# Hybrid decoder layer on one core: the first four weight tiles accumulated together by k tile from a packed array

## The chip, the cores and the metric

The kernel runs on one core of a Trainium2 chip. The metric is the time of one execution on the device in microseconds (us); the time of a version is the median of its runs. The engines are named as the profile names them: PE (TensorE's matmuls), PEld (its weight loads), DVE (VectorE), ACT (ScalarE), POOL (GpSimd) and SP, whose queue issues most DMAs.

## The reference

One decoder layer on x of 512 tokens by 1024 channels: a SwiGLU half-step, two token mixers side by side, cross-attention to a memory of 256 rows, a second SwiGLU half-step and a final norm. What matters here is the first line and the compression in the mixer:

```python
def swiglu(h, w_gate, w_up, w_down):
    return (jax.nn.silu(h @ w_gate) * (h @ w_up)) @ w_down

x = x + 0.5 * swiglu(rms_norm(x, norm_ffn1[l]), w1_gate[l], w1_up[l], w1_down[l])
...
    def compress(a, pe, w1, w2):
        blocks = a[:, tok] + pe[None, None, :, None, :]
        flat = blocks.transpose(0, 1, 3, 2, 4).reshape(B, n_cmp, G, CMP_BLOCK * HEAD_DIM)
        return jax.nn.gelu(flat @ w1) @ w2
```

D_FF is 2816, so gate and up have 22 tiles of 128 columns each. All is float32.

## The kernel before

Activations lie transposed: `x[k]`, k = 0 to 7, holds 128 channels by 512 tokens. Each float32 operand is split into a high part and a low remainder (`h` and `l`), and a product is the sum of three matmuls: high by high, high by low, low by high. A split takes one ACT copy (`h`) and one DVE subtraction (`l = src - h`). Weights arrive in raw tiles `wr` (3 buffers) and are split into pairs `wh`, `wl` (2 buffers of 128 x 1024); `wload` does load and split, and `dense` runs the matmuls of one output tile, k by k, into a PSUM bank. Bank tag "d" has three buffers, "s" and "t" two, "o" one.

The norm's factor is applied after the products: ACT multiplies x by the gain only (`xh`, `xl`), and the factor `rb`, one per token, comes from `Norm`: squares on ACT (`sq`), their sum on DVE (`acc`), column sums on PE (L189), a square root on ACT (L206), four small matmuls that spread it over the partitions (L218), and a copy (L221).

`ffn` first runs `nstd` standard feature tiles (6 in the first half-step, 4 in the second): gate tile f, then up tile f, 24 matmuls each. In the first half-step the loads of gate tile 0, up tile 0 and x are written out by hand on SP's queue (L146, L139), in pieces, since no work can start before them. Behind a gate tile DVE multiplies by `rb` (`t1`, L310), ACT takes silu, DVE multiplies by `rb` once more (L313), and behind the up tile DVE makes `act` (L316). `prepare` (after the tiles in `PREP`) makes the operands for the other 16 tiles, which `seven` runs as pairs of tiles with seven products of half the size each. Ahead of `seven` stand four filler matmuls into banks that nobody reads (L408). `seven` begins with the splits of pair 0: `h1` (1024 columns from the raw tile `r1`), the sum `s2`, then `h2` (two halves of 512). Its first product reads the first 512 columns of `h1`, its second the first 512 of `h2`, its third the second half of `h2`, its fourth the second half of `h1`.

In the mixer, `compress_in` makes a projection tile and spreads it over `F` with eight DVE additions, `fh` and `fl` being their splits; `keys` makes a projection tile and its splits `kkh`, `kkl`. They run in the order compress_in(0), compress_in(1), keys(3), keys(2), keys(4), and after them the value projection `vcat` (L726) fills three banks "d" and one "o". A bank "d" comes free when DVE has read it (`q32` in compress_in, printed as q; `zg` in keys).

The instructions between `ordered()` keep the order in which they are written. The rest is ordered by a scheduler at build time that goes by priorities; each engine then runs its own list strictly in order.

## Time and profile before

| what | value |
|---|---|
| median of 3 runs | 1271.76 us (1271.66 to 1272.06) |
| the profiled execution, its own time | 1270.87 us |
| its span from the first to the last instruction | 1268.9 us |
| PE busy | 1250.5 us, 99% of the span |
| DVE busy | 839.4 us, 66% |
| ACT busy | 664.7 us, 52% |
| granted TensorE clock, mean | 0.998 |
| mean DMA rate | 131 GB/s |

The profile is of one execution. Its own time stands 2.0 us above its span, and 0.9 us below the median of the runs. Matmuls are pipelined, so the busy time of one overlaps the next; how fast PE goes is read from the distance of two starts.

### The profile page before, as it was taken

How to read it: one execution, taken by the hardware profiler on the slowest of the kernel's cores; microseconds unless marked ns; L12 is line 12 of the kernel's file. 1: busy time of each engine (PE TensorE's matmuls, PEld its weight loads, DVE VectorE, ACT ScalarE, POOL GpSimd, SP SyncE). 2: the span in 40 equal slices, each digit the busy share in tenths (PEclk: the TensorE clock that was granted, in tenths of full speed). 3: DMA queues.
4: the chain of work that ended last, by engine and by line, in shares of the span. 5: the costliest groups of instructions: out<-in, count | busy, mean ns of one | idle time of the engine just before them, and what ended most of it. 6: DMA issues, size and time to landing. Idle time of an engine off the chain costs nothing.

```text
span 1268.9 us, 19130 instructions
## 1 busy us (share of the span) xinstructions
PE 1250.5 (99%) x7324; PEld 1092.2 (86%) x7324; DVE 839.4 (66%) x1642; ACT 664.7 (52%) x1309; POOL 74.8 (6%) x101
## 2 busy tenths in 40 slices
PE   7999999999999999999999999999999999999997
PEld 5889999987888788888888898887889999998887
DVE  5867676744357888787878666555687777674224
ACT  6345555632234777777785454444445545553223
POOL 0101110003010000000001000000001111100000
PEclk9999999999999999999999999999999999999999
DMA  5727767237542522222224335211446766623233
GB/s 186 192 81 205 187 175 191 86 121 222 179 157 90 183 80 75 88 65 72 64 91 149 134 128 188 81 53 67 125 132 163 184 189 190 181 80 99 86 102 112
DMA packets 58939, 166.01 MB, mean 131 GB/s; under 512 B 6264, under 2 KB 6784, under 8 KB 58848
## 3 DMA queue, kind: packets, MB, share of 16 engines
q1 hardware_dynamic: 44240, 129.16, 30.6%
q0 software_dynamic: 14032, 34.57, 12.6%
q8 instruction: 57, 0.93, 0.3%
q10 hardware_dynamic: 576, 1.07, 0.2%
q14 instruction: 34, 0.28, 0.1%
HBM read 160.54 MB, written 10.07 MB: 134 GB/s over the span
## 4 chain that ended last, share of the span: by engine, by line
PE 96%; DVE 2%; DMA 1%; issue 0%; ACT 0%; SPq 0%; DVEq 0%
PE ps_d L127 47%; PE ps_d L75 12%; PE ps_t L75 8%; PE ps_d L500 5%; PE ps_o L75 4%; PE ps_s L75 4%; PE ps_d L978 4%; PE ps_d L1132 2%; PE ps_t L863 1%; PE ps_s L776 1%; PE ps_o L771 1%; PE ps_s L775 1%; PE ps_o L770 1%; PE ps_d L726 1%; PE ps_o L1191 1%; PE ps_s L1165 1%
## 5 line engine op out<-in xcount | busy, mean ns | idle before, releaser
L102 ACT ACTIVATE wh<-wr 128x512 fp32r<-128x512 f32 (+3 forms) x257 | 170.0, 695 | 299.6 <-PE ps_d L127 154.1
L103 DVE TENSOR_TENSOR wl<-wr,wh 128x512 fp32r<-128x512 f32 (+3 forms) x257 | 191.9, 771 | 136.9 <-ACT wh L102 135.3
L127 PE MATMUL ps_d<-xh,wh 128*128 128x512 f32 x456 | 182.3, 401 | 7.3 <-ACT xh L75 7.3
L127 PE MATMUL ps_d<-xh,wl 128*128 128x512 f32 x456 | 183.3, 402 | 0.8 <-DVE wl L103 0.8
L127 PE MATMUL ps_d<-xl,wh 128*128 128x512 f32 x456 | 182.2, 400 | 0.2 <-DVE xl L75 0.2
L127 PEld LDWEIGHTS ps_d<-xh,wh 128*128 128x128 f32 x456 | 86.3, 189 | 25.8 <-ACT xh L75 9.1
L127 PE MATMUL ps_d<-al,wh 128*128 128x512 f32 (+1 forms) x286 | 107.8, 377 | 0.0
L127 PE MATMUL ps_d<-ah,wh 128*128 128x512 f32 (+1 forms) x286 | 107.8, 377 | 0.0
L127 PE MATMUL ps_d<-ah,wl 128*128 128x512 f32 (+1 forms) x286 | 107.7, 376 | 0.0
L127 PEld LDWEIGHTS ps_d<-xl,wh 128*128 128x128 f32 x456 | 86.3, 189 | 19.1 <-DVE xl L75 1.8
L127 PEld LDWEIGHTS ps_d<-xh,wl 128*128 128x128 f32 x456 | 86.4, 189 | 18.7 <-DVE wl L103 1.3
L75 DVE TENSOR_TENSOR wl<-wr,wh 128x1024 fp32r<-128x1024 f32 (+3 forms) x46 | 49.6, 1085 | 27.5 <-ACT wh L75 27.5
L127 PEld LDWEIGHTS ps_d<-al,wh 128*128 128x128 f32 x286 | 53.8, 188 | 10.6
L127 PEld LDWEIGHTS ps_d<-ah,wh 128*128 128x128 f32 x286 | 53.8, 188 | 10.5
L127 PEld LDWEIGHTS ps_d<-ah,wl 128*128 128x128 f32 x286 | 53.8, 188 | 10.4
L75 DVE TENSOR_TENSOR h4l<-r,h4h 128x1024 fp32r<-128x1024 f32 x34 | 41.7, 1226 | 19.5 <-ACT h4h L75 19.5
L75 DVE TENSOR_TENSOR h2l<-s,h2h 128x512 fp32r<-128x512 f32 x68 | 44.0, 687 | 14.0 <-ACT h2h L75 13.8
L75 PE MATMUL ps_d<-t,h4h 128*128 128x256 f32 x272 | 50.5, 283 | 0.0
L75 PE MATMUL ps_d<-n,h2h 128*128 128x256 f32 x272 | 50.4, 283 | 0.0
L75 PE MATMUL ps_o<-t,h2h 128*128 128x256 f32 x272 | 50.3, 283 | 0.0
L75 PE MATMUL ps_t<-n,h3h 128*128 128x256 f32 x272 | 49.9, 282 | 0.0
L75 PE MATMUL ps_t<-b,h4h 128*128 128x256 f32 x272 | 49.9, 281 | 0.0
(348 smaller groups left out, 3144.1 us busy)
## 6 DMA issues: line engine op xcount, KB each, us to landing
wr<-in_w_down_dram SPq DMA_DIRECT2D x34, 512.0 KB, 3.5
wr<-in_w_in_dram SPq DMA_DIRECT2D x29, 512.0 KB, 3.5
wr<-in_w_gate_dram SPq DMA_DIRECT2D x26, 512.0 KB, 5.2
wr<-in_w_up_dram SPq DMA_DIRECT2D x26, 512.0 KB, 5.8
s<-in_w_gate_dram SPq DMA_DIRECT2D x17, 512.0 KB, 5.1
s<-in_w_gate_dram POOLq DMA_DIRECT2D x17, 512.0 KB, 5.9
s<-in_w_up_dram SPq DMA_DIRECT2D x17, 512.0 KB, 5.0
s<-in_w_up_dram POOLq DMA_DIRECT2D x17, 512.0 KB, 5.8
```

The lines of the kernel that those rows point to most:

```text
L75: return lambda *args, **kw: tc.keep_in_program_order(call(*args, **kw))
L102: A.activation(h, src, AF.Copy)
L103: V.tensor_sub(l, src, f32(h))
L127: yield T.matmul(out, w[:, c], m, start=i == 0, stop=i == total - 1)
L500: T.matmul(two[m], w[:, cc], v, start=f == 0 and z == 0, stop=f == FT - 1 and z == 2)
L726: T.matmul(pv[i][:, :VC], m[k][:, tk], ww[:, w], start=k == 0 and z == 0, stop=k == KT - 1 and z == 2)
L770: T.matmul(po[:, cols], w, h[:, src], start=start, stop=False, skip_group_check=True)
L771: T.matmul(po[:, cols], w, l[:, src], start=False, stop=False, skip_group_check=True)
L775: first = T.matmul(out, q[:, tk], kk[0][:, ks], start=True, stop=False)
L776: T.matmul(out, q[:, tk], kk[1][:, ks], start=False, stop=True)
L978: yield T.matmul(pj, w[:, c], m, start=n == 0, stop=n == 11)
L1132: T.matmul(pj[t], m[k][:, tk], ww[:, w], start=k == 0 and z == 0, stop=k == KT - 1 and z == 2)
```

## The change

Four edits, cut to their core below. First, gate tiles 0 and 1 and up tiles 0 and 1 come from one array `w1_first`, four raw tiles of 128 x 1024, each with two k tiles of all four; they are accumulated k by k into two banks "d" and two "s", 12 matmuls for each k. x tiles are loaded between the packed tiles. Second, nine matmuls on a tile of zeros (`WARM`) go ahead of them. Third, `PREP` of the first half-step goes from (1, 3) to (2, 4), since tiles 0 and 1 now end together. Fourth, two orders: `seven` splits pair 0 by halves in the order in which products read them, in both half-steps, and keys(3) goes between the two compress_in.

```diff
-PREP = {"1": (1, 3), "2": (0, 1)}
+PREP = {"1": (2, 4), "2": (0, 1)}
 NEARLY = 4
+WARM = 9
...
-    load_w(0, 0, 256)
+    def load_w(i, c0=0, c1=1024):
+        if c0 == 0:
+            raw0.append(raw_tile())
+        nc.sync.dma_start(raw0[i][:, c0:c1], a["w1_first"][i][:, c0:c1])
+
+    load_w(0, 0, 512)
     load_x(0)
-    load_w(1, 0, 256)
+    load_w(0, 512, 1024)
     load_x(1)
-    load_w(0, 256, 1024)
-    load_x(2)
-    load_w(1, 256, 1024)
-    for k in range(3, KT):
-        load_x(k)
+    for i in range(1, 4):
+        load_w(i)
+        load_x(2 * i)
+        load_x(2 * i + 1)
...
-            pg, pu = bank("d"), bank("d")
-            fg, fu = first if first and f == 0 else (None, None)
-            dense(pg, [(wsrc["g"][f], KT)], xh, xl, fg, step=1024)
+            if first and f < 2:
+                pg, pu = first[2 * f:2 * f + 2]
+            else:
+                pg, pu = bank("d"), bank("d")
+                dense(pg, [(wsrc["g"][f], KT)], xh, xl, step=1024)
...
-            dense(pu, [(wsrc["u"][f], KT)], xh, xl, fu, step=1024)
+            if not (first and f < 2):
+                dense(pu, [(wsrc["u"][f], KT)], xh, xl, step=1024)
...
         def seven():
-            h1(0)
+            d = q_[0]
+            a_, b_ = slice(0, 512), slice(512, 1024)
+            d["h1"], d["h2"] = wpair(), hl("h2", 1024)
+            split(*(t[:, a_] for t in d["h1"]), d["r1"][:, a_])
+            split(*(t[:, a_] for t in d["h2"]), d["s"][:, a_])
             s2(0)
-            h2(0)
+            split(*(t[:, b_] for t in d["h2"]), d["s2"])
+            split(*(t[:, b_] for t in d["h1"]), d["r1"][:, b_])
...
+        warm = pool.tile([P, 1], F32R, name="warm")
         with ordered():
-            part(0, 0, 256)
+            V.memset(f32(warm), 0.0)
+            for _ in range(WARM):
+                T.matmul(bank("t"), warm.to_broadcast([P, P]), warm.to_broadcast([P, S]), start=True, stop=True)
+            first = [bank(n) for n in "ddss"]
             for k in range(KT + 4):
                 if k < KT:
-                    scale_split(xh[k], xl[k], x[k], gain(0, k))
-                    if k < 3:
-                        part(*((1, 0, 256), (0, 256, 1024), (1, 256, 1024))[k])
+                    if k % 2 == 0:
+                        h, l = wpair()
+                    cols = ((0, 512), (512, 1024))[k % 2] if k < 2 else (0, 1024)
+                    if k < 2 or k % 2 == 0:
+                        c = slice(*cols)
+                        A.activation(h[:, c], raw0[k // 2][:, c], AF.Copy)
+                    A.activation(xh[k], x[k], AF.Copy, scale=gain(0, k))
+                    if k < 2 or k % 2 == 0:
+                        V.tensor_sub(l[:, c], raw0[k // 2][:, c], f32(h[:, c]))
+                    V.scalar_tensor_tensor(xl[k], x[k], gain(0, k), f32(xh[k]), op0=ALU.mult, op1=ALU.subtract)
+                    for z, (w, m) in enumerate(((h, xh), (l, xh), (h, xl))):
+                        for t in range(4):
+                            o = k % 2 * 512 + t * P
+                            T.matmul(first[t], w[:, o:o + P], m[k], start=k == 0 and z == 0,
+                                     stop=k == KT - 1 and z == 2)
...
         compress_in(0)
+        kkw = keys(3)
         compress_in(1)
-        kkw = keys(3)
```

How the built programs stand, at three places. First the head of PE's list. Before, it is gate tile 0, three matmuls for each k tile of x (xh_92 and xl_100 are the two parts of x tile 0, xh_93 of tile 1):

```order
L127 MATMUL ps_d<-xh_92,wh 128x512
L127 MATMUL ps_d<-xl_100,wh 128x512
L127 MATMUL ps_d<-xh_92,wl 128x512
L127 MATMUL ps_d<-xh_93,wh 128x512
L127 MATMUL ps_d<-xl_101,wh 128x512
L127 MATMUL ps_d<-xh_93,wl 128x512
L127 MATMUL ps_d<-xh_94,wh 128x512
```

The same place now (xh_95 and xl_103 are the parts of x tile 0, xh_96 of tile 1):

```order
L76 MATMUL ps_t<-warm 128x512 x9
L76 MATMUL ps_d<-xh_95,wh 128x512 x2
L76 MATMUL ps_s<-xh_95,wh 128x512 x2
L76 MATMUL ps_d<-xh_95,wl 128x512 x2
L76 MATMUL ps_s<-xh_95,wl 128x512 x2
L76 MATMUL ps_d<-xl_103,wh 128x512 x2
L76 MATMUL ps_s<-xl_103,wh 128x512 x2
L76 MATMUL ps_d<-xh_96,wh 128x512 x2
```

Nine matmuls on zeros have come in front, and there are 12 matmuls instead of 3 for each k tile. The column sums of the norm (L189, now L191) stood behind 52 matmuls of the first tiles and stand now behind all 96 of tiles 0 and 1. On SP's list the fourth packed tile stands behind x tile 7. One of the four fillers of the first half-step (L408, now L413) has gone forward into gate tile 3, where it stands behind that tile's second matmul.

Second, DVE at the start of `seven` in the first half-step, before:

```order
L316 TENSOR_TENSOR act<-ps_d,s_668 128x512
L75 TENSOR_TENSOR wl<-wr,wh 128x1024
L75 TENSOR_TENSOR s_719<-s_512,wr 128x512
L75 TENSOR_TENSOR h2l<-s_512,h2h 128x512
L75 TENSOR_TENSOR h2l<-s_719,h2h 128x512
```

and now:

```order
L321 TENSOR_TENSOR act<-ps_d,s_685 128x512
L76 TENSOR_TENSOR wl<-wr,wh 128x512
L76 TENSOR_TENSOR h2l<-s_529,h2h 128x512
L76 TENSOR_TENSOR s_740<-s_529,wr 128x512
L76 TENSOR_TENSOR h2l<-s_740,h2h 128x512
L76 TENSOR_TENSOR wl<-wr,wh 128x512
```

The subtraction of 1024 columns that stood in front of the first product is now two of 512, and the second stands behind the splits of `h2`.

Third, DVE in the mixer, from the evacuation of compress_in(1) (q_3785) to the second `zg`, before:

```order
L627 TENSOR_TENSOR q_3785<-ps_d,rb 128x512
L103 TENSOR_TENSOR wl<-wr,wh 128x512
L103 TENSOR_TENSOR fl<-F,fh 128x4x64
L103 TENSOR_TENSOR wl<-wr,wh 128x512
L103 TENSOR_TENSOR fl<-F,fh 128x4x64
...
L636 TENSOR_TENSOR F<-q_3785,pe 64x8x31 x2
L696 TENSOR_TENSOR zg<-ps_d,rb 128x512
L103 TENSOR_TENSOR fl<-F,fh 128x4x64 x2
L103 TENSOR_TENSOR wl<-wr,wh 128x512
L705 TENSOR_TENSOR kkl<-zg,kkh 64x512
```

and now, from the first `zg`:

```order
L719 TENSOR_TENSOR zg<-ps_d,rb 128x512
L104 TENSOR_TENSOR wl<-wr,wh 128x512
L104 TENSOR_TENSOR fl<-F,fh 128x4x64
L104 TENSOR_TENSOR wl<-wr,wh 128x512
L104 TENSOR_TENSOR fl<-F,fh 128x4x64
L728 TENSOR_TENSOR kkl<-zg,kkh 64x512
...
L650 TENSOR_TENSOR q_3851<-ps_d,rb 128x512
L104 TENSOR_TENSOR wl<-wr,wh 128x512
L659 TENSOR_TENSOR F<-q_3851,pe 64x8x31 x6
```

The work of keys(3) (`zg`, `kkl`) now stands ahead of the second compression (q_3851), and the first half of the `wl` of keys(4) (the one behind q_3851) ahead of that compression's additions. From the first q to the third `zg` the same operations stand in both lists.

## Rows read from the trace of the kernel before

**Rows 1.** The page: the span, and PE's busy time.

```profile
span 1268.9 us, 19130 instructions
...
PE 1250.5 (99%) x7324; PEld 1092.2 (86%) x7324; DVE 839.4 (66%) x1642; ACT 664.7 (52%) x1309; POOL 74.8 (6%) x101
```

**Rows 2.** Waits of PE, whole span: waiter, releaser, us in total, times, longest.

```profile
PE ps_d L127 <- ACT xh L75: 7.3, 3, 4.8
PE ps_d L75 <- DVE wl L75: 1.5, 2, 0.8
PE ps_d L726 <- DVE zg L696: 1.0, 1, 1.0
PE ps_d L127 <- DVE wl L103: 0.8, 1, 0.8
```

**Rows 3.** Timeline of PE, 0 to 25 us: start, us, operation, count, idle before.

```profile
4.82 0.80 PE L127 MATMUL ps_d<-xh,wh 128*128 128x512 f32 x1 [4.82 <-ACT xh L75]
...
11.28 0.80 PE L127 MATMUL ps_d<-xh,wh 128*128 128x512 f32 x1 [1.68 <-ACT xh L75]
...
14.62 0.61 PE L127 MATMUL ps_d<-xh,wl 128*128 128x512 f32 x1
15.05 0.41 PE L127 MATMUL ps_d<-xl,wh 128*128 128x512 f32 x1
...
24.17 0.95 PE L189 MATMUL ps_t<-ones,acc 128*128 128x1 f32 x8
```

**Rows 4.** Busy time by stretch, line 127 alone; counts in brackets.

```profile
0.00:24.16 24.16, 16.65 (x52) 11.02 (x52) 1.00 0.62 206
```

**Rows 5.** The chain that ended last, one piece: start, us, count.

```profile
28.43 52.73 PE ps_d L127 x226
```

**Rows 6.** Timeline of ACT, 0 to 36 us.

```profile
3.17 0.42 ACT L75 ACTIVATE wh<-wr 128x256 fp32r<-128x256 f32 x1 [0.71 <-DMA wr<-in_w_gate_dram]
4.04 0.72 ACT L75 ACTIVATE xh<-x,gains 128x512 fp32r<-128x512 f32 x1 [0.46 <-DMA x<-in_x_dram]
4.77 0.42 ACT L75 ACTIVATE wh<-wr 128x256 fp32r<-128x256 f32 x1
6.82 0.72 ACT L75 ACTIVATE xh<-x,gains 128x512 fp32r<-128x512 f32 x1 [1.63 <-DMA x<-in_x_dram]
9.77 0.84 ACT L75 ACTIVATE wh<-wr 128x768 fp32r<-128x768 f32 x1 [2.23 <-DMA wr<-in_w_gate_dram]
...
11.66 0.84 ACT L75 ACTIVATE wh<-wr 128x768 fp32r<-128x768 f32 x1 [0.44 <-DMA wr<-in_w_up_dram]
...
20.16 1.07 ACT L102 ACTIVATE wh<-wr 128x1024 fp32r<-128x1024 f32 x1 [0.41 <-PE ps_d L127]
23.20 1.06 ACT L102 ACTIVATE wh<-wr 128x1024 fp32r<-128x1024 f32 x1 [1.97 <-PE ps_d L127]
...
28.47 0.60 ACT L221 ACTIVATE rb<-ps_t 128x512 f32<-128x512 f32 x1 [2.64 <-PE ps_t L218]
```

**Rows 7.** By stretch, all engines: PE, PEld, DVE, ACT, POOL, clock, DMA share, GB/s.

```profile
4.75:9.75 5.00, 4.01 (x6) 1.58 (x6) 1.84 (x3) 1.16 (x3) 0.00 (x0) 1.00 0.82 226
9.75:14.85 5.10, 3.33 (x7) 2.18 (x8) 3.93 (x6) 4.64 (x8) 0.00 (x0) 1.00 1.05 407
```

**Rows 8.** Timeline of DVE, 24 to 50 us.

```profile
29.10 0.69 DVE L310 TENSOR_TENSOR t<-ps_d,rb 128x512 f32<-128x512 f32 x1 [2.47 <-ACT rb L221]
...
32.89 1.22 DVE L103 TENSOR_TENSOR wl<-wr,wh 128x1024 fp32r<-128x1024 f32 x1
```

**Rows 9.** Timeline of DVE, 76 to 86 us, at the start of `seven`.

```profile
81.19 0.69 DVE L316 TENSOR_TENSOR act<-ps_d,s 128x512 f32<-128x512 f32 x1 [2.96 <-PE ps_d L127]
81.80 1.22 DVE L75 TENSOR_TENSOR wl<-wr,wh 128x1024 fp32r<-128x1024 f32 x1
```

**Rows 10.** Timeline of DVE, 374 to 400 us, in the mixer.

```profile
374.95 0.69 DVE L627 TENSOR_TENSOR q<-ps_d,rb 128x512 f32<-128x512 f32 x1 [0.22 <-ACT rb L221]
...
398.63 0.69 DVE L696 TENSOR_TENSOR zg<-ps_d,rb 128x512 f32<-128x512 f32 x1
```

More of the change, by code (lines that the diff above doesn't have):

```diff
@@ L117, in wload, with dense_steps @@
         return h, l
-    def dense_steps(out, chunks, mh, ml, first=None, step=STEP):
+    def dense_steps(out, chunks, mh, ml, step=STEP):
         total = 3 * sum(n for _, n in chunks)
@@ L122, in dense_steps @@
         for src, n in chunks:
-            h, l = first or wload(src, n * P, step)
+            h, l = wload(src, n * P, step)
             for kk in range(n):
@@ L139, in load_x @@
         nc.sync.dma_start(x[k], a["x"][k * P:(k + 1) * P, :])
-    raw0 = [raw_tile(), raw_tile()]
-    src0 = [a["w1_gate"][0], a["w1_up"][0]]
+    raw0 = []
     gains = g.tile([P, 6 * KT], F32, name="gains")
     nc.scalar.dma_start(gains, a["gains"])
-    def load_w(i, c0, c1):
-        nc.sync.dma_start(raw0[i][:, c0:c1], src0[i][:, c0:c1])
-    load_w(0, 0, 256)
+    def load_w(i, c0=0, c1=1024):
[3 more added lines that the diff above has]
+    load_w(0, 0, 512)
     load_x(0)
-    load_w(1, 0, 256)
+    load_w(0, 512, 1024)
     load_x(1)
-    load_w(0, 256, 1024)
-    load_x(2)
-    load_w(1, 256, 1024)
-    for k in range(3, KT):
-        load_x(k)
+    for i in range(1, 4):
+        load_w(i)
+        load_x(2 * i)
+        load_x(2 * i + 1)
     ident = g.tile([P, P], F32, name="ident")
@@ L530, in hybrid_layer @@
     with tc.tile_pool(name="f1", bufs=1, reuse_waits="tile") as pool:
-        first = [wpair(), wpair()]
-        def part(i, c0, c1):
-            h, l = first[i]
-            split(h[:, c0:c1], l[:, c0:c1], raw0[i][:, c0:c1])
         n1 = Norm(S, "x", tsq=("E", NE), tacc=("E", NE))
+        warm = pool.tile([P, 1], F32R, name="warm")
         with ordered():
-            part(0, 0, 256)
+            V.memset(f32(warm), 0.0)
+            for _ in range(WARM):
+                T.matmul(bank("t"), warm.to_broadcast([P, P]), warm.to_broadcast([P, S]), start=True, stop=True)
+            first = [bank(n) for n in "ddss"]
             for k in range(KT + 4):
                 if k < KT:
-                    scale_split(xh[k], xl[k], x[k], gain(0, k))
-                    if k < 3:
-                        part(*((1, 0, 256), (0, 256, 1024), (1, 256, 1024))[k])
+                    if k % 2 == 0:
[13 more added lines that the diff above has]
+                                     stop=k == KT - 1 and z == 2)
                 if k >= 4:
@@ L1299, in _layout @@
         out[f"w{t}_down"] = _tiles(f[f"w{t}_down"][0])
+    w1 = np.stack([out[f"w1_{n}"][t].reshape(P, KT, P) for t in range(2) for n in ("gate", "up")], axis=2)
+    out["w1_first"] = w1.reshape(P, 4, 1024).transpose(1, 0, 2)
     w = f["w_in"][0]
```

## The prediction, made before the changed kernel had run

> **What bounds the kernel now.** I read the page first. PE is busy for 1250.5 of 1268.9 us [rows 1], so a change gains only where PE stands still or goes slowly, and loses only where it makes PE wait. The view of PE's waits says where it stands still [rows 2]: 7.3 us in three waits for `xh` at the very start, 1.5 us in two waits for a `wl` (one at the start of each `seven`), 1.0 us for `zg` and 0.8 us for `wl` in the mixer. All four places are places that the change edits.
>
> The view of waits does not show slowness, so I went on to the timeline of PE [rows 3]. Two starts there lie 0.43 us apart (14.62 and 15.05), and in the long piece of the chain 226 matmuls of the same shape take 52.73 us, 0.2333 us each [rows 5]. Up to about 15 us PE therefore runs at the lower of its two clock levels (512 columns in 0.43 us is 1.2 GHz), after it at the higher, 2.4 GHz. The stretch view prints 1.00 for these early stretches too; the distances of the starts decide here.
>
> Both losses go into one number, which I call the lead-in: the time at which PE reaches a point, less 0.2333 us for each real matmul behind it. The column sums start at 24.17 us [rows 3], behind 52 matmuls [rows 4], so the lead-in of before is 24.17 - 52 x 0.2333 = 12.04 us. Any start that brings PE to full speed with a smaller lead-in gains the difference to the end, as long as PE stays the bound.
>
> **The start, costed.** What sets the new lead-in is when data lands, and when ACT has made `wh` and `xh` of it. SP's list has the same kind of loads as before, so I read when the n-th KB was there from ACT's timeline, where the waits for DMA end [rows 6]: 128 KB at 3.17 us, 384 at 4.04, 512 by 4.77, 768 at 6.82, 1152 at 9.77, 1792 at 11.66. Between them I interpolate. The slow middle is a low DMA rate, 226 GB/s against 407 later [rows 7].
>
> k = 0 needs 256 KB of weights (3.60) and x tile 0 (512 KB in all, 4.77); `xh` takes 0.72, so PE starts real work near 5.5 us, against 4.82 before. k = 1 needs 1024 KB in all: 6.82 + 256/384 x 2.95 = 8.79, plus 0.72 for `xh` and 0.06 to PE (as from 4.76 to 4.82 before): 9.57. With 12 matmuls behind it that is a lead-in of 9.57 - 2.80 = 6.77. k = 2 needs the second packed tile, 1536 KB in all: 9.77 + 384/640 x 1.89 = 10.90; its `wh` takes 1.07 (the 1024-wide copy at 20.16), then `xh` of tile 2, landed by 11.66, another 0.72 and 0.06: 12.75, a lead-in of 12.75 - 24 x 0.2333 = 7.15. From here data comes at 407 GB/s, 512 KB in 1.3 us, while PE takes 2.80 us for the 12 matmuls that use them, and nothing binds later: the fourth packed tile, behind x tile 7 on SP's queue, is at 4096 KB, 11.66 + 2304 KB at 407 GB/s = 17.5 us; its `wh` must wait for the pair buffer that k = 3 gives up near 18.3, and PE wants it at 7.15 + 72 x 0.2333 = 23.9. So the new lead-in is **7.15 us, a gain of 4.9 us**. Its bounds: 5.5, if data never binds after k = 0, and one microsecond more for each microsecond by which the 1536th KB slips; I take the rows.
>
> The nine matmuls on zeros take 9 x 0.43 = 3.9 us at the lower level. They wait for a memset of one column only. If they start by 1.6 us, they end before 5.5 and cost nothing, since PE has no data; a later start would be paid one for one. What they are worth is the clock. Before, the rise at 15.05 came 3.8 us after the matmul at 11.28, the last long wait [rows 3]. If the nine count, the higher level is there near 5 us and k = 0 ends by 8.4, well ahead of the data of k = 1. If the pause between them and k = 0 spoils it, the rise comes at 5.5 + 3.8 = 9.3: nine matmuls at 0.43, three at 0.23, k = 0 ends at 10.1, k = 1 at 12.9, and the lead-in is 7.3. Between these two the nine matmuls are worth 0.15 us, so it hardly matters which holds.
>
> **What the start makes late.** The norm's factor `rb` now follows all 96 matmuls. Before, the `wh` copy at 23.20 waited for PE, and the square root behind it on ACT and all of the chain led to `rb` at 29.07, 5.87 us later [rows 6]. Now the copy that stands there waits for the end of k = 7: 7.15 + 96 x 0.2333 = 29.6 us, and `rb` comes near 35.5. PE meanwhile does gate tile 2 in the third bank "d" (29.6, plus 0.8 each for sums and spreading, plus 5.6: to 36.8). Up tile 2 needs the bank of gate tile 0, which DVE reads first after `rb`, done at 36.2: 0.6 us to spare. Gate tile 3 (from 42.4) needs its `wl` at 43.1, behind the filler that the scheduler put there. DVE has ten operations between `rb` and that `wl`; six took 32.89 - 29.10 = 3.79 us, 0.63 each [rows 8], so 35.5 + 6.3 + 1.22 = 43.0. It fits with nothing left; I charge no wait, with 0.5 us as its bound. The later steps have a microsecond to spare. The filler moved out of the cover in front of `seven` and costs its 0.23 us.
>
> **`seven`.** In the first half-step DVE makes `act` at 81.19 when PE ends the last up tile, and the 1024-wide `wl` behind it takes 1.22 us [rows 9]; the third matmul of the first product waits 0.76 for it (the longest of these two is printed as 0.8 [rows 2]). Half as wide an operation takes 0.69, so PE goes on 0.53 us sooner. The second half of `h2` then has to be ready 2.6 us after that, and by 0.69 for each DVE step it is, with 0.2 us to spare. The second half-step has the same wait: 2 x 0.53 = **1.06 us gained**, at least 0, at most 1.5.
>
> **The mixer.** The 0.8 us wait for `wl` goes, since the first half of that `wl` stands 4 us earlier. But the wait for `zg`, the last in these rows, ends with a chain on DVE alone: from the first `q` at 374.95 to the end of the third `zg` at 399.32 [rows 10], 24.4 us of DVE work in which it waits for nothing worth 0.5 us. The new order has the same operations between these two points. PE comes 0.8 us sooner to the same bank and waits 0.8 us longer: **0 us**, between 0.3 lost and 0.8 gained.
>
> **Sum.** Against the profiled 1270.87 us: -4.9 + 0.23 - 1.06 + 0 = -5.7, so 1265.1. The median of the runs stood 0.9 above that execution, so I predict 1266.0.
>
> **Rivals.** *The clock does not rise at the start.* If waits between k steps hold PE at the lower level until 15.05, as they did before with 0.8 and 1.7 us of waiting, 22 matmuls are done by then (5.5 + 22 x 0.43), and the lead-in is 15.05 - 22 x 0.2333 = 9.9: 1268.8 us. Against it: 3.9 us of matmuls stand ahead, 12 in a row per k at the lower level outlast the data, and the waits of 0.8 to 1.0 us later in the run left the level high. Chance 0.10. The Trainium skill has this case in "TensorE: Matmul & The Clock Gate", section "HAM oscillation — how this bites in real kernels": a k loop whose matmuls per step are shorter than the wait for the next slice falls back to the lower clock at each step. By that rule the start would be this rival; the trace of before agrees with it up to 15 us and shows nothing for steps of 12.
>
> *A later wait takes back a part.* `rb`, the tight `wl` of gate tile 3 or the tight `h2` makes PE wait 0.5 to 2.5 us: 1266.5 to 1268.5. For it speak margins of 0.1 to 0.6 us; against it that each is paid once. Chance 0.14.
>
> *Slower.* It is the bank of gate tile 0: up tile 2 cannot start until DVE has read it behind `rb`. Each microsecond of `rb` beyond 36.1 is paid. To eat 5.7 us and to be 0.2% (2.5 us) slower, `rb` must come after 44.3, nine later than worked out. Only an ACT or DVE list that waits in a circle with PE would do it: 1274. Chance 0.03.
>
> *More than forecast.* Data lands as fast as later (lead-in 5.5), or the mixer's wait goes too: 1264.0. Chance 0.08.
>
> **How the numbers follow.** The forecast has 0.65, with its own range of 1265.0 to 1267.2 from the landing times by half a microsecond either way and from the 0.5 us at gate tile 3. 8 in 10 reaches to the clock rival above and to the better case below: 1264.2 to 1268.6. Faster by over 0.2% (below 1269.2; 0.2% is about what a measurement of this kernel can tell from no change): all of the forecast and the better case, most of the first two rivals, 0.88; same 0.09; slower 0.03.
>
> **What would show it.** PE's first real matmul near 5.5 us, a wait near 1 us before k = 1 and a short one before k = 2, distances of 0.23 from k = 1 on, the sums near 29.6. `rb` near 35 and no wait in 36 to 45. The waits at both `seven` down from 0.8 to about 0.2 to 0.5. In the mixer one wait of 1.5 to 1.8 for `zg` in place of two. A slip of the packed tiles' landing, or a wait behind `rb`, would make it wrong.

## The result: 1263.8 us, 2.2 us below the forecast

The changed kernel takes 1263.84 us (median of 6 runs, 1263.66 to 1264.10), the kernel before 1271.45 (median of 6, 1271.04 to 1272.06): a ratio of 0.9940, 95% interval 0.9927 to 0.9953. The gain of 7.6 us is real. It lies 0.36 us below the lower end of the range that was given, 1264.2, and 2.16 below the predicted 1266.0. Between the two profiled executions the gain is 1270.87 - 1263.74 = 7.13 us.

The profile after, in the views of [rows 1] and [rows 2]. First the page:

```profile
span 1261.7 us, 19148 instructions
...
PE 1249.8 (99%) x7333; PEld 1092.7 (87%) x7333; DVE 838.8 (66%) x1644; ACT 664.1 (53%) x1310; POOL 74.8 (6%) x101
```

PE's busy time is all but the same as before. The gain is in waits and in slow products, not in less work: what was idle or half-speed before is now done at full speed, while the nine products on zeros count as busy too. Then PE's waits:

```profile
PE ps_d L749 <- DVE zg L719: 1.5, 1, 1.5
PE ps_d L76 <- ACT xh L76: 1.2, 2, 0.8
PE ps_t L76 <- DVE warm L76: 1.0, 1, 1.0
PE ps_d L76 <- DVE wl L76: 0.7, 2, 0.5
```

Of 7.3 us for `xh` 1.2 are left, of 1.5 at the two `seven` 0.7, and in the mixer one wait of 1.5 stands where two of 1.0 and 0.8 were. The timeline of PE shows the same places one by one, and the points from which the gain is measured:

```profile
0.95 3.80 PE L76 MATMUL ps_t<-warm 128*128 128x512 f32 x9 [0.95 <-DVE warm L76]
5.50 0.73 PE L76 MATMUL ps_d<-xh,wh 128*128 128x512 f32 x2 [0.75 <-ACT xh L76]
...
8.40 0.63 PE L76 MATMUL ps_d<-xh,wh 128*128 128x512 f32 x2
...
11.84 0.73 PE L76 MATMUL ps_d<-xh,wh 128*128 128x512 f32 x2 [0.48 <-ACT xh L76]
...
28.75 0.95 PE L191 MATMUL ps_t<-ones,acc 128*128 128x1 f32 x8
...
77.11 0.39 PE L76 MATMUL ps_d<-b,wl 128*128 128x256 f32 x1 [0.45 <-DVE wl L76]
...
232.73 0.39 PE L510 MATMUL ps_d<-ah,wh 128*128 128x512 f32 x1
...
359.70 0.39 PE L128 MATMUL ps_d<-ah,wl 128*128 128x512 f32 x1
...
392.84 0.46 PE L749 MATMUL ps_d<-wh,xh 128*128 128x408 f32 x1 [1.49 <-DVE zg L719]
...
946.40 0.39 PE L76 MATMUL ps_d<-b,wl 128*128 128x256 f32 x1 [0.23 <-DVE wl L76]
```

From the first real product at 5.50 us to 28.75, pairs of products start 0.47 us apart: the higher clock level all through. The sums stand behind 96 real products, so the lead-in is 28.75 - 96 x 0.2333 = 6.35 us, against 12.04 before [rows 3, 4]: 5.69 us of the gain.

Each of these numbers is of one execution. Nine of the experiments below leave the start as it is here; in the ten traced executions of it, the lead-in runs from 5.7 to 7.1 us, 6.2 on average. The old start has two, with 12.0 and 13.2 us. A difference of half a microsecond between the starts of two traces therefore proves little by itself.

If the two PE streams are laid beside each other product by product, the gain is 5.66 us ahead of the first `seven`, 5.97 behind its wait, 7.35 at the end of the half-size products, 6.29 at the end of the first down projection, 6.54 behind the mixer's wait, 7.12 behind the second `seven`'s wait, 7.06 at the last product.

Between the sums and the first `seven` PE waits nowhere that the view prints. The rows of ACT for the start and for `rb`:

```profile
6.42 0.73 ACT L76 ACTIVATE xh<-x,gains 128x512 fp32r<-128x512 f32 x1 [0.28 <-DMA x<-in_x_dram]
9.56 1.06 ACT L76 ACTIVATE wh<-wr 128x1024 fp32r<-128x1024 f32 x1 [2.41 <-DMA wr<-in_w_first_dram]
11.07 1.33 ACT L76 ACTIVATE xh<-x,gains 128x512 fp32r<-128x512 f32 x2 [0.46 <-DMA x<-in_x_dram]
...
33.77 0.60 ACT L223 ACTIVATE rb<-ps_t 128x512 f32<-128x512 f32 x1 [2.23 <-PE ps_t L220]
```

`rb` is ready at 34.37 (35.5 was forecast). x tile 1 is there at 6.4 us where 8.79 was forecast, the second packed weight tile at 9.56 where 10.90 was.

### The profile page after: what moved, and what is told of

Same layout as the page of the kernel before. It is cut to its first block, busy times and chain, and to the rows that moved or that the text cites. A ratio compares the mean times of both kernels' runs of the same rounds, so it can differ in the third digit from the quotient of the medians.

```text
span 1261.7 us, 19148 instructions
## 1 busy us (share of the span) xinstructions
PE 1249.8 (99%) x7333; PEld 1092.7 (87%) x7333; DVE 838.8 (66%) x1644; ACT 664.1 (53%) x1310; POOL 74.8 (6%) x101
## 3 DMA queue, kind: packets, MB, share of 16 engines
q10 hardware_dynamic: 576, 1.07, 0.2%
## 4 chain that ended last, share of the span: by engine, by line
PE 96%; DVE 2%; DMA 1%; ACT 0%; issue 0%; SPq 0%; DVEq 0%
PE ps_d L128 45%; PE ps_d L76 12%; PE ps_t L76 8%; PE ps_d L510 5%; PE ps_s L76 4%; PE ps_o L76 4%; PE ps_d L1001 4%; PE ps_d L1155 2%; PE ps_t L886 1%; PE ps_s L799 1%; PE ps_o L794 1%; PE ps_s L798 1%; PE ps_o L793 1%; PE ps_d L749 1%; PE ps_o L1214 1%; PE ps_s L1188 1%
## 5 line engine op out<-in xcount | busy, mean ns | idle before, releaser
L128 PE MATMUL ps_d<-xh,wl 128*128 128x512 f32 x424 | 169.9, 401 | 0.1
L128 PE MATMUL ps_d<-xh,wh 128*128 128x512 f32 x424 | 168.8, 398 | 0.0
L128 PE MATMUL ps_d<-xl,wh 128*128 128x512 f32 x424 | 168.5, 397 | 0.0
L128 PEld LDWEIGHTS ps_d<-xh,wl 128*128 128x128 f32 x424 | 79.9, 188 | 16.4 <-DVE wl L104 0.5
L128 PEld LDWEIGHTS ps_d<-xl,wh 128*128 128x128 f32 x424 | 79.8, 188 | 15.9
L128 PEld LDWEIGHTS ps_d<-xh,wh 128*128 128x128 f32 x424 | 79.9, 189 | 15.4
L76 DVE TENSOR_TENSOR wl<-wr,wh 128x1024 fp32r<-128x1024 f32 (+1 forms) x49 | 52.2, 1071 | 29.3 <-ACT wh L76 29.3
L76 PE MATMUL ps_d<-b,wh 128*128 128x256 f32 x272 | 49.8, 282 | 0.0
```

Of the source, the lines that this page charges most:

```text
L76: return lambda *args, **kw: tc.keep_in_program_order(call(*args, **kw))
L128: yield T.matmul(out, w[:, c], m, start=i == 0, stop=i == total - 1)
```

## The experiments

All but two are edits of the changed kernel. Where no number of runs is given it is four or five. Medians are compared with its 1263.84, spans of the profiled execution with its 1261.7; "ratio" is that of the times to the kernel before, timed beside each. Not tried alone are the order by k tile without the rest, and the new `PREP`.

**Without the nine products on zeros.** Are they worth the 0.15 us of the prediction?

```diff
-WARM = 9
+WARM = 0
```

> The nine products on a tile of zeros ahead of the first real one are left out; all the rest, the addresses too, stays. Theory (the zero products bring the clock up): with them the clock rose 3.0 us after PE began (0.95 to 3.98), so without them it should rise about 3 us after the first real product, near 8.5 us; some 6.5 products done by then in place of 13 cost 1.5 us, of which the wait of 0.48 us that PE now has ahead of k tile 2 takes back a part: the sum L191 starts 1.0 us later (29.8), the time is near 1264.9. Rival 1 (the pauses of the start keep the clock low, as in the kernel before, where it rose 10.2 us after PE began): rise near 15, sum L191 about 3.5 to 4.5 us later, 1267.5 to 1268.5. Rival 2 (the loads alone set the lead-in of 6.35 us): no difference, 1263.9.

Measured: 1265.11 us, ratio to before 0.9951 (0.9939 to 0.9964); span 1263.0. PE's start:

```profile
5.53 1.22 PE L76 MATMUL ps_d<-xh,wh 128*128 128x512 f32 x2 [5.53 <-ACT xh L76]
...
8.25 1.05 PE L76 MATMUL ps_s<-xh,wl 128*128 128x512 f32 x2
9.10 0.81 PE L76 MATMUL ps_d<-xl,wh 128*128 128x512 f32 x2
9.75 0.64 PE L76 MATMUL ps_s<-xl,wh 128*128 128x512 f32 x2
...
29.82 0.95 PE L191 MATMUL ps_t<-ones,acc 128*128 128x1 f32 x8
```

Pairs are 0.85 us apart up to 9.1 and 0.47 from 9.75 on, so the clock rises near 9.5, one microsecond later than expected here and close to the 9.3 that the prediction gave for nine products that do not count. The sums come at 29.82 as expected, 1.07 us later, and the median is 1.27 higher. The theory holds in size; both rivals fall. The nine are worth about 1.1 us and not 0.15, because the wait for the data of k = 1, which was to hide the slow products, is not there.

**The same nine products in the kernel before.** What do they bring without the order by k tile?

```diff
+        warm = pool.tile([P, S], F32R, tag="E", name="warm", bufs=NE)[:, :1]
         with ordered():
+            V.memset(f32(warm), 0.0)
+            for _ in range(9):
+                T.matmul(bank("t"), warm.to_broadcast([P, P]), warm.to_broadcast([P, S]), start=True, stop=True)
             part(0, 0, 256)
```

> The kernel before with one addition: the nine products on a tile of zeros ahead of its first product (the tile takes a buffer of tag E, all addresses stay). Theory (in the kernel before the clock comes up late and at another moment in each execution: 15.05 us in one profiled execution, 17.8 in another of the same start, which put PE 0.9 us apart; that is what lets its times spread from 1270.2 to 1273.0 and its median stand 0.9 above its profiled execution): with the clock up before the first real product the times spread by less than 1.0 us, the median stands within 0.3 us of the profiled execution, and the 12 products of 11.28 to 15.05 us at half speed are worth 1.0 to 1.5 us, with the median's 0.9 some 2 us: near 1269.4. Rival (the spread and the 0.9 have another cause, such as pauses in the mixer or the loads): times spread by 2 us or more as before, median 1270.2 to 1270.7.

Measured: 1271.80 us (11 runs, 1270.60 to 1272.88), ratio to before 1.0001 (0.9992 to 1.0010): nothing. The theory falls. PE's timeline and the stretch view (PE, PEld, DVE, ACT, POOL, granted clock, DMA share, GB/s) say why:

```profile
6.02 0.39 PE L127 MATMUL ps_d<-xh,wl 128*128 128x512 f32 x1
7.73 0.51 PE L127 MATMUL ps_d<-xh,wh 128*128 128x512 f32 x1 [1.31 <-ACT xh L75]
```

```profile
6.00:8.00 2.00, 0.69 (x3) 0.19 (x1) 0.29 (x1) 0.72 (x1) 0.00 (x0) 1.00 0.72 207
8.00:10.00 2.00, 1.41 (x3) 0.46 (x2) 0.46 (x1) 0.82 (x2) 0.00 (x0) 0.65 0.99 310
10.00:12.00 2.00, 1.06 (x2) 0.56 (x3) 1.85 (x3) 1.74 (x4) 0.00 (x0) 0.50 1.05 398
12.00:14.00 2.00, 2.00 (x5) 1.51 (x6) 2.00 (x4) 2.00 (x4) 0.00 (x0) 0.50 1.06 414
14.00:16.00 2.00, 2.00 (x7) 1.59 (x6) 2.00 (x5) 2.00 (x5) 0.00 (x0) 0.65 1.03 410
```

The clock was up at 6.0 us (a product there takes 0.39 us, as at the higher level); then PE, with three products per k tile, had work for 0.69 of the 2 us from 6 to 8, and the granted clock fell to 0.50 at 8.6 us and stayed there until 15.4. This is the first rival of the prediction, in the old start. The Trainium skill's "TensorE: Matmul & The Clock Gate", section "HAM oscillation — how this bites in real kernels", describes a like case: steps shorter than the wait for the next slice fall back each time. This run agrees in kind: three products are 0.70 us of work at the higher level, the idle time behind them was 1.31 us, and in the next step the clock fell, once and for several steps. The changed kernel, with twelve products a step, does not fall back. The nine products need the order by k tile behind them. And since the clock fell again here, the run cannot decide what spreads the times of the kernel before.

**POOL's small loads later.** Why does data land slowly up to 10 us?

```diff
-                G.dma_start(tb["rel"], a["rel"])
-                G.dma_start(pe, a["pe"])
-                G.dma_start(rowm, a["rowm"])
-                G.dma_start(sinks, a["sinks"].to_broadcast([P, 8]))
+                with ordered():
+                    G.dma_start(tb["rel"], a["rel"])
+                    G.dma_start(pe, a["pe"])
+                    G.dma_start(rowm, a["rowm"])
+                    G.dma_start(sinks, a["sinks"].to_broadcast([P, 8]))
```

> POOL's four small loads (rel, pe, rowm, sinks; 454 packets under 512 bytes with gains and ident aside) are issued behind the first FFN's weight loads of POOL in place of at 2 to 4 us. Theory (they hold up the start's loads: in 8 to 10 us the DMA engines are 97% busy and move only 191 GB/s): the second weight tile lands near 8 us in place of 9.53 and x2 near 9 us in place of 11.04, PE's wait of 0.48 us ahead of k tile 2 and the 0.7 us of the first k tiles' late operands go, lead-in 5.3 to 5.9 in place of 6.35: -0.5 to -1.0 us, 1262.8 to 1263.3. Rival (the loads land late by their place in the queue, whatever else is moved): landings within 0.3 us of those now, 1263.8.

Measured: 1263.13 us, ratio 0.9935 (0.9922 to 0.9947). One row of the stretch view of the changed kernel, and the same one here:

```profile
8.00:10.00 2.00, 2.00 (x10) 1.63 (x9) 0.00 (x0) 0.44 (x1) 0.00 (x0) 1.00 0.97 191
```

```profile
8.00:10.00 2.00, 2.00 (x10) 1.57 (x10) 0.78 (x2) 1.42 (x3) 0.00 (x0) 1.00 1.05 414
```

With equally busy DMA engines more than twice as much data moves once the four loads are gone. This is no accident of one execution: from 8 to 10 us the eleven traces of this order of loads that have the four there show 143 to 222 GB/s, the two without them (this one and that of the last experiment) 414 and 413. PE:

```profile
8.51 0.63 PE L76 MATMUL ps_d<-xh,wh 128*128 128x512 f32 x2
...
11.31 0.63 PE L76 MATMUL ps_d<-xh,wh 128*128 128x512 f32 x2
...
28.11 0.95 PE L191 MATMUL ps_t<-ones,acc 128*128 128x1 f32 x8
```

The wait of 0.48 ahead of k = 2 is gone and the lead-in is 5.71 in place of 6.35: 0.64 us, 0.71 by the medians. The lead-in alone would lie within its spread from execution to execution; the times do not overlap (1262.98 to 1263.57 against 1263.66 to 1264.10). The theory holds for the time and the rate, and only in part for the landings: the second weight tile is there at 8.88, where near 8 was expected, and x tile 1 lands no sooner than with the loads (its `xh` starts at 7.57; in the ten executions with them at 6.4 to 7.9). So the four loads are not what sets x tile 1. Nor do they make up the 454 small packets of the expectation: the first 40 us have 592 packets under 512 bytes with them and 480 without.

The Trainium skill's "DMA: Bandwidth & Descriptors", section "Rules for kernel authors", says that transfers under 64 KB are mostly overhead and should be joined. That is about the small transfers themselves; that four of 0.5 to 32 KB slow the large ones beside them is what the two rows show.

**The old order of the splits at `seven`.**

```diff
-            d["h1"], d["h2"] = wpair(), hl("h2", 1024)
-            split(*(t[:, a_] for t in d["h1"]), d["r1"][:, a_])
-            split(*(t[:, a_] for t in d["h2"]), d["s"][:, a_])
-            s2(0)
-            split(*(t[:, b_] for t in d["h2"]), d["s2"])
-            split(*(t[:, b_] for t in d["h1"]), d["r1"][:, b_])
+            h1(0)
+            s2(0)
+            h2(0)
```

> Only the splits of the first half-size products stand in their old order again (all of h1, s2, all of h2), in both FFNs. Theory (PE waits there for the last of these splits): the wait for act or wl at some 77 us grows from 0.45 to about 0.76 us and the one at 946 us from 0.23 to about 0.75, together +0.8 to +1.1 us: 1264.6 to 1264.9. Rival (the new order only moves the wait to a later product, or the 0.3 us at the first place are only the fillers' count): 0.0 to +0.3 us, 1263.8 to 1264.1.

Measured: 1265.48 us, ratio 0.9950 (0.9938 to 0.9963); span 1262.9. PE's waits:

```profile
PE ps_d L76 <- DVE wl L76: 1.9, 2, 1.2
```

1.9 us in place of 0.7, and the span is 1.2 longer; the median is 1.6 higher, above the 0.8 to 1.1 that was expected. The reorder is worth 1.2 us of waits, and the theory holds in kind. The wait at 77 us grows to 1.16 and not to 0.76: the filler that has moved away from there explains 0.23 of these 0.40 us, the rest stays open.

**Both reordered pieces alone,** in the kernel before (its diff is the inverse of the last and the next one).

> The kernel before with only the two reordered pieces (splits of the first half-size products, compression inputs); its start is the old one. Theory (the parts add up: 7.1 us between the two profiled executions, of which the splits are 1.24 by the waits, the compression order 0.2 to 0.3): 1.2 to 1.5 us faster than the kernel before, some 1270.1. Rival (the splits' gain needs the new start, since the fillers ahead of them and prepare stand elsewhere there): 0.0 to 0.6 us faster.

Measured: 1270.08 us (11 runs), ratio 0.9989 (0.9981 to 0.9998): some 1.4 us faster, as the theory has it, though the interval (0.3 to 2.4 us) does not shut out the upper end of the rival. PE's waits decide:

```profile
PE ps_d L731 <- DVE zg L701: 1.5, 1, 1.5
PE ps_d L75 <- DVE wl L75: 0.4, 2, 0.2
```

The two `seven` wait 0.4 us in place of 1.5 [rows 2] and the mixer once for 1.5 in place of 1.8 in two waits: some 1.4 us together. The splits need no new start. The profiled execution brought something else. Its start is that of before, but:

```profile
17.38 0.62 PE L127 MATMUL ps_d<-xh,wh 128*128 128x512 f32 x1
17.80 0.43 PE L127 MATMUL ps_d<-xl,wh 128*128 128x512 f32 x1
18.07 0.39 PE L127 MATMUL ps_d<-xh,wl 128*128 128x512 f32 x1
```

Here starts lie 0.42 us apart up to 17.8, where the kernel before had changed level at 15.05 [rows 3]. PE is 1.1 us later behind this point than in the profile of before.

**The old order of the compression inputs.**

```diff
         compress_in(0)
-        kkw = keys(3)
         compress_in(1)
+        kkw = keys(3)
```

> Only the compression inputs stand in their old order again (both inputs ahead of the first keys). Theory (DVE works without a pause from 374 to 392 us and has the same work in either order, so the end of it sets when PE goes on): waits of 0.82 and 0.96 us in place of one of 1.49, so +0.2 to +0.3 us, 1264.0 to 1264.1. Rival (the first of the two waits was really saved): +0.8 us, 1264.6.

Measured: 1263.94 us, ratio 0.9940 (0.9926 to 0.9953); span 1262.2.

```profile
PE ps_d L749 <- DVE zg L719: 1.0, 1, 1.0
...
PE ps_d L128 <- DVE wl L104: 0.8, 1, 0.8
```

Two waits, 1.78 us together, in place of one of 1.49: 0.3 us by the waits; the 0.1 by the medians is within their spread and decides nothing. By the waits the theory holds; the 0.8 us of the first wait were not saved but spent 8 us later.

**ACT copies the keys' low parts.** Does relief for DVE shorten that wait?

```diff
-                V.tensor_copy(l[oth], f32(l[own]))
+                A.activation(l[oth], f32(l[own]), AF.Copy)
```

> The copies of the low parts of the keys to the other half (CAST kkl<-kkl, 0.42 us each, four of them between 378 and 392 us) are done by ACT in place of DVE. Theory (the wait of 1.49 us at 392.84 us is the end of a chain on DVE): the chain gets 1.6 us shorter, the wait all but goes, -1.2 to -1.5 us: 1262.3 to 1262.6. Rival (ACT, which does the keys' high parts, becomes the late one, or the next bank is waited for in its place): 0.0 to -0.4 us, 1263.4 to 1263.8.

Measured: 1263.81 us, ratio 0.9939 (0.9927 to 0.9952). The rival's time, and neither's reason: the wait for `zg` is gone, as the theory has it, but

```profile
PE ps_d L128 <- DVE wl L104: 1.7, 1, 1.7
```

stands at 386.02 us. The scheduler, given another set of operations, put this split of weights behind all eight adds of the compression input (it ends at 386.0; in the changed kernel it stands ahead of them and is done at 381.4).

**The same, with the second input behind both pairs of keys** (on the layout of addresses that is described last, whose own time is 1255.46).

```diff
         compress_in(0)
         kkw = keys(3)
-        compress_in(1)
         kks = keys(2, wide, 32)
+        compress_in(1)
```

> The one with h2, h3 and h4 at 64 and the rest at 0 (1255.5 us), and besides ACT copies the keys' low parts and the second compression input stands behind both pairs of keys. Theory (the wait of 1.5 us at 392.84 was the end of a chain on DVE, and what moved it to 386 us in the earlier try was a split of weights placed behind six adds of the compression input): neither wait is left, -1.2 to -1.5 us, 1254.0 to 1254.3. Rival (DVE's sum of work over this stretch keeps one wait of about 1.5 us wherever the pieces stand): 1255.2 to 1255.5.

Measured: 1258.49 us, ratio to before 0.9902 (0.9889 to 0.9916), 3 us worse than without. The wait:

```profile
PE ps_d L752 <- DVE zg L722: 2.9, 1, 2.9
```

And the stretch view around it:

```profile
384.00:388.00 4.00, 2.71 (x13) 2.05 (x12) 3.87 (x9) 0.94 (x3) 0.00 (x0) 1.00 0.00 0
388.00:392.00 4.00, 2.35 (x10) 2.30 (x11) 3.57 (x8) 3.68 (x8) 0.00 (x0) 0.85 0.44 118
392.00:396.00 4.00, 4.00 (x18) 3.93 (x17) 0.78 (x2) 2.35 (x5) 0.00 (x0) 0.72 0.29 118
```

Both sides of the expectation fall. DVE now waits 2.5 us for ACT (0.90, 0.97 and 0.63 us between 376 and 382), the wait for `zg` doubles, and behind it the granted clock falls to 0.85 and 0.72. A wait that grew by 1.4 us cost 3, and the two rows at 0.85 and 0.72 account for the rest: 0.15 and 0.28 of 4 us each are 1.7. What the least possible wait is here stays open.

**Addresses back.** The column of zeros got 32 bytes of its own at the front of the first FFN's pool and moved all other tiles of the pool by them. Does that matter?

```diff
-        warm = pool.tile([P, 1], F32R, name="warm")
+        warm = pool.tile([P, S], F32R, tag="E", name="warm", bufs=NE)[:, :1]
```

> The tile of zeros takes a buffer of tag E in place of 32 bytes of its own, so every tile of the first FFN's pool is back at the addresses (remainder 32 by 128) that it has in the kernel before. Theory (the pace of products depends on the address of the operands): down projection products on the tiles with f from 15 on are spaced 227 ns apart again in place of 233.5, the 256-wide products into ps_t about 118.8 in place of 115.9; over the first FFN -1.0 us and +1.35 us, so +0.35 us on the time: 1264.2. Rival (the spacings differ from kernel to kernel or run to run for another reason): 233.5 and 115.9 stay, 0.0 us.

Measured: 1264.47 us (1263.65 to 1266.59), ratio 0.9947 (0.9933 to 0.9960). The time alone can't tell 0.35 us, the trace can:

```profile
77.22 0.38 PE L76 MATMUL ps_d<-b,wl 128*128 128x256 f32 x1 [0.45 <-DVE wl L76]
...
234.27 0.40 PE L510 MATMUL ps_d<-ah,wh 128*128 128x512 f32 x1
...
360.17 0.39 PE L128 MATMUL ps_d<-ah,wl 128*128 128x512 f32 x1
```

From the first wait of `seven` to the first down product 157.05 us, in the changed kernel 155.62: +1.43. From there to the last down product 125.90, in the changed kernel 126.97: -1.07. With the same instructions, in the same order. The theory holds, net 0.36 us.

**All tiles moved by 32 bytes,** the weights too.

```diff
+    g.tile([P, 8], F32, name="pad")
     ps = ctx.enter_context(tc.tile_pool(name="ps", bufs=1, space=PSUM))
```

> 32 unused bytes at the front of the outermost pool: all tiles move by 32 bytes. The tiles of tag B, operands of most products, go from remainder 0 to 32 (by 128), the weights wh and wl from 32 to 64, the first FFN's own tiles to 96, the second's to 64. Theory 1 (products are spaced 227 ns where the moving operand stands at remainder 32): nearly all of some 2,900 products of 512 columns on tag B go from 233.5 to 227 ns: -15 to -19 us, near 1246. Theory 2 (227 ns where moving operand and weights have the same remainder): only the second FFN's 168 products with f from 15 on do so, as now: within 0.5 us of now but for the half-size products. Rival (no effect of addresses): 1263.8, spacings as now.

Measured: 1263.95 us, ratio 0.9940 (0.9928 to 0.9953); theory 1 falls. What counts is not an address by itself. By the trace the spacings are those of the changed kernel (down products 233.3 ns in the first FFN, 227.3 in the second), as theory 2 and the rival both have it, so this run does not tell them apart.

**Three more layouts,** by unused bytes ahead of `wh` and `wl` (32, 96, 96) and, in the third, 64 ahead of `h2`, `h3` and `h4`; the column of zeros is in tag E in all.

```diff
     V.memset(ones, 1.0)
+    g.tile([P, 24], F32, name="pad")
...
+            if i == 0:
+                pool.tile([P, 16], F32, name="pad")
             ys = []
```

> 32 unused bytes ahead of the weights' tiles wh and wl, and the tile of zeros in a buffer of tag E: wh, wl and both FFNs' own tiles go to remainder 64 (by 128), the tiles of tag B stay at 0. Theory (a product is spaced closer where the remainders by 64 of weights and moving operand agree: down products on tag E had 32 and 32 and 227 ns in the kernel before, 32 and 64 and 233.5 ns after): now all products of wh and wl on tag B agree too (64 and 0) and some 2,900 products of 512 columns go from 233.5 to near 227 ns, -15 to -19 us, near 1246; the half-size products of h4 on tag B are at 113.6 ns in both FFNs. Rival 1 (only the distance of the second pool's tiles from the weights counts, by something larger than 64 or 128 bytes): first FFN's down products back at 227 ns, h4 on b back at 118.5 or kept at 113.6, the others unchanged, 1263.0 to 1264.3. Rival 2 (no effect of the addresses): all spacings as in the changed kernel, 1263.8.

> 96 unused bytes ahead of the weights' tiles and the tile of zeros in a buffer of tag E: tag B, wh, wl and both FFNs' own tiles all stand at remainder 0 by 128. Theory (read from the traces so far: products of 512 columns are spaced 227.5 ns where moving operand and weights have the same remainder by 128 and 233 otherwise, those of 256 columns 119.5 with the same, 118.2 at a distance of 32, 113.5 to 114.6 at 64): 2,231 products of 512 columns -5.5 ns each, -12.4 us, the first FFN's down products on tag E -1.0, some 1,470 products of 256 columns +1.3 ns and 191 +6 ns each, +3.1: -10.3 us, 1253.5. Rival (59 products at 0 and 0 in an earlier run had 230.6 ns): half of that, -3 to -4 us, 1260. Rival 2 (what helps is something else than the remainders): 1262 to 1264.

> As the one with all at remainder 0, and 64 unused bytes ahead of the tiles h2, h3 and h4 of both FFNs, so that these weights of the half-size products stand at 64, while their moving operands stand at 0. Theory (256 columns want a distance of 64, 512 columns none): beside the -13.4 us of the products of 512 columns, some 1,660 products of 256 columns on h2, h3, h4 go from 119.4 to 114 (-9.0 us), 190 of b on h4 from 118.5 to 113.5 (-0.9), 1,090 of b on wh and wl from 118.2 to 119.5 (+1.5): -21.8 us, 1242. Rival (DVE and ACT, which split the weights, become what the half-size products wait for): -13 to -17 us, 1247 to 1251.

Measured: 1258.50 us (ratio 0.9897, 0.9883 to 0.9910), 1263.95 (0.9940, 0.9928 to 0.9953) and 1255.46 (0.9873, 0.9859 to 0.9886). The table has the mean distance of starts of neighbouring products in ns, worked out from the traces, by the remainder by 128 of the addresses of moving operand and weights (first and second number), with the count:

```
kernel             512 columns                             256 columns
changed            0/32: 233.1 (2231)  32/32: 227.8 (235)  0/32: 118.1 (1378)  32/32: 119.6 (899)  64/64: 119.1 (763)  0/64: 113.5 (191)
32 ahead of wh     0/64: 233.3 (2226)  64/64: 227.9 (404)  0/64: 114.6 (1566)  64/64: 119.2 (1662)
96 ahead of wh     0/0:  231.9 (2773)                      0/0:  119.2 (3231)
96, and 64 at h2   0/0:  231.9 (2778)                      0/0:  118.7 (1204)  0/64: 115.1 (2059)
```

As forecasts all three miss: near 1246, 1253.5 and 1242 were expected. The first layout lies far below both rivals of its expectation, the second has the time of its second rival, the third gains 8.4 us where 21.8 was the theory and 13 to 17 the rival. Still the addresses alone are worth 8.5 us between the second layout and the third, which differ in nothing but the 64 bytes.

For 256 columns a distance of 64 between the remainders helps: 113.5 to 115.1 ns on average, against 119 with none. That is where the third layout has most of its 8.4 us under the changed kernel: the half-size products of both FFNs take 348.1 in place of 354.8 us. But the mean of 115.1 hides two groups. At the same remainders 0/64 the products on `h2` and those of `t` on `h4` are at 113.5 to 114.2 ns, those of `n` on `h3` and `b` on `h4` at 117.3 to 117.8; and `b` on `h4`, again at 0/64, had 113.4 in the first layout. So the remainder by 128 is not the whole rule here either. For 512 columns the theory falls: with equal remainders the 2,229 products on tag B are at 232.6 ns, and only the 404 on tiles outside tag B at 228.0. Some other property of the tiles must come in for both sizes, which stays open.

**The best layout with the late small loads.**

> The same with POOL's four small loads behind the first FFN's. Theory (the two gains are in different stretches, so they add): 0.7 us below the one without, 1241.3. Rival: no difference to the one without.

Measured: 1255.37 us, ratio 0.9870 (0.9855 to 0.9886), the rival's side: the two gains do not add. By the traces PE is 0.3 to 0.5 us ahead from 39 to 400 us and 0.3 to 0.5 behind from 435 us on. Between them stands a wait of 0.4 us for a `wh` (L679, at 422.8 us) that the layout without late loads does not have; why was not tried. At some 1255.4 us both run 8.4 us below the changed kernel and 16.3 below the kernel before (1271.72 beside them).

## Why the prediction was wrong by 2.2 us

**The start: right mechanism, a term mis-sized.** Clock, order and the memset column went as forecast, with the first real product at 5.50 us. The step that failed is the landing times: "Between them I interpolate", by the KB in front of a load, and from it "a lead-in of 12.75 - 24 x 0.2333 = 7.15". x tile 1 came 2.4 us sooner than its KB said, the second packed tile 1.3; over the ten traced executions of this start they came 0.9 to 2.4 and 0.6 to 2.3 us sooner. The lead-in was 6.35, so the gain 5.69 in place of 4.9: 0.8 us (7.15 is just above the latest of the ten lead-ins).

Two things were wrong with the reading. The KB in front of a load are not what has been moved when it lands. In the kernel before, x tile 1 ends the first 768 KB and was there at 6.82 us; the DMA queues up to that time:

```profile
q1 hardware_dynamic: 709, 1.13, 54.9%
```

SP's queue had begun 1.13 MB by then, and the 768 KB are 0.79 of these: the rest belonged to later loads, so the bytes do not land load after load. And the slow stretch of the old traffic, behind which the second packed tile was put, was in good part, judging by the run without them (414 in place of 191 GB/s from 8 to 10 us), the work of the four small loads of POOL. Why x tile 1 comes as early as it does is not shown: in the two runs without the small loads it came at 7.57 and 6.92, inside the 6.4 to 7.9 of the ten executions with them.

**The step of the nine products** ("worth 0.15 us") failed with it: it rested on PE having no data for k = 1 until 9.57. The `xh` of k = 1 was ready at 7.15, and PE took it up at 8.40 without a wait, as soon as k = 0 was done. The nine are worth 1.1.

**What the start makes late: right.** `rb` at 34.37 and no wait from 29 to 77 us. The `wl` of gate tile 3 was made between 40.6 and 41.8 us, and PE did not wait for it.

**`seven`: right.** -0.53 + 0.23 for the filler was forecast for the first half-step, -0.53 for the second; the waits went from 0.76 to 0.45 (-0.31) and from 0.75 to 0.23 (-0.52).

**The mixer: right in kind.** One wait in place of two, 0.3 us shorter by the waits and 0.25 by PE's positions; 0 was forecast, with 0.8 as the bound.

**Not in the sum: the addresses.** They were put at nothing without a word. 0.36 us were gained in the first FFN.

Against the profiled execution of before the forecast was -5.73 us. Lead-in 0.8, addresses 0.36 and mixer 0.25 make the difference to the -7.13 that came.

**The last step failed too:** "The median of the runs stood 0.9 above that execution", added to the changed kernel as if whatever makes these 0.9 stayed there. The changed kernel's median stands 0.10 above its own profiled execution, so 0.8 us of the 2.16 are from here. The distance is not a property of a kernel: it is the place of one execution among its kernel's runs, and in these experiments it went from -0.74 (both reordered pieces alone) to +0.90 (the nine products in the kernel before).

What spreads the times is suggested, not shown. The two traced executions of the old start took the clock up at 15.05 and at 17.8 us, with lead-ins of 12.0 and 13.2, so the one that the forecast was built on was the quicker of the two. The new start is not free of this: over its ten executions the clock rose between 3.8 and 6.3 us and the lead-in went from 5.7 to 7.1. The execution with 7.1 (all tiles moved by 32 bytes) is the slowest of its five runs, while the 6 runs of the changed kernel lie within 0.44 us and the 5 with the addresses back over 2.9. The run that was to show the cause in the old start lost its clock again.

Of the rivals, "more than forecast" (1264.0, chance 0.08) has the time that came, and that is partly luck: its lead-in of 5.5 was not reached, its mixer's wait did not go, and the addresses and the median's distance, which it does not have, filled the rest. The clock rival was real, but for the old start.

## What to carry to other kernels

Do not read a landing time off by the bytes in front of a load, and look first at what else is on the DMA engines in a slow stretch: here four loads of 0.5 to 32 KB halved the rate of the large ones. A warm-up by empty products was worth 1.1 us where the work behind it kept PE busy, and nothing where it did not. A profiled execution is one draw: trace a start more than once before a lead-in goes into a sum, and do not carry the distance between median and profiled execution to another kernel.

## What the runs showed of the chip that was not expected

- The pace of a product depends on where its operands lie in SBUF, relative to each other. Moving the tiles by 32 bytes changed 256-column products of `b` on `h4` from 118.5 to 113.6 ns, 512-column down products on tag E from 227 to 233.5. The layout found best gains 8.4 us by unused bytes alone, though the rule behind it is not known: at the same remainders by 128, 256-column products were at 113.5 ns on some tiles and at 117.8 on others.
- The granted clock fell within the run as well: behind a wait of 2.95 us for `zg` to 0.72 in the following stretch, while behind the waits of 1.5 at the same place it stays at 1.00.
- Two executions of the old start took PE's clock up 2.7 us apart, ten of the new one up to 2.4.
